# A two-layer streaming encoder step: both halves of the normalised tokens kept in DRAM, gate blocks tied to the state steps, and the last third of the modulation product moved into the state stage

## The chip, the cores and the metric

The kernel runs on one core of one Trainium2 chip. The metric is the device time of one launch in microseconds, as the median of several runs. A profiled execution shows in addition what each engine did: PE is TensorE (matmul), PEld its weight load, DVE is VectorE, ACT is ScalarE, POOL is GpSimd, and SP is SyncE, which here only issues transfers. A transfer can also be issued from ACT's or POOL's own instruction stream.

## The reference: what is computed

2176 tokens (a prompt of 2048, and 8 samples of 16) of width 1024 go through two layers in float32. Each layer computes

```
mod = silu(c) @ w_ada[i] + b_ada[i]        # shift, scale, gate of 1024 each; 9 rows of c
h   = rms_norm(x, norm_g[i]) * (1 + scale) + shift
x   = x + gate * branch_i(h)
```

Layer 0 is a diagonal complex state-space branch (S5): `u, z = split(h @ w_in)`; u goes through a complex recurrence (64 groups of 16 channels, 64 states each), then a GELU, a gated product `y * sigmoid(y @ w_glu + b)`, a multiplication by `silu(z)`, and `@ w_out`. Layer 1 is a gated delta rule on chunks of tokens, with a short convolution ahead of it and a gated output product behind it. A last RMSNorm ends the step. z is called the gate half here: its columns of `w_in` are the second 1024.

## The kernel before

**Split products.** A float32 matrix product is made of three matmuls at the faster float32r rate: every operand is split into a high part (a rounding copy, by ACT) and a low part (the difference, by DVE), and `mm3` (L145 to L152) issues high times high, high times low, low times high (lines L149, L150, L151). Some small products stay in plain float32: the modulation product `ada`, and in the state stage the transposes `abT`, the kernels `pk`, the inputs `pb` and the Toeplitz part of `py`.

**Tiling.** Tokens are cut into 8 blocks of 272 columns (`NCH`). Weights are cut into 8 output blocks of 128 columns, each holding 8 tiles of 128x128. One output block of one token block is 8 x 3 = 24 matmuls of 128x128 by 128x272.

**Stages**, in time order. In stage A, for each token block j, the tokens are loaded, normalised, modulated and split into the tiles `hh` and `hl`; 8 output blocks of u (`pd`) are computed and stored to `u_d`. The normalised and modulated tokens `xt` themselves are stored to `h0_d` in one transfer. Stage A also computes the modulation product: the 6144 columns are done in three groups of 2048 (`ada0`, `ada1`, `ada2`), each in 8 steps over the 1024 rows of `w_ada` (`ada_steps`, L172). A step has four matmuls of 128x32 by 128x512, one for each quarter of the group's columns, and each writes another 32 rows of one PSUM tile, through another quarter of the PE array (`tile_position=(0, 32 * j)`).

In stage B, the S5 recurrence runs in 16 state steps b (four channel groups each: `s5_setup`, `s5_load`, `s5_main`): PE makes `abT`, `pk`, `pb` and `py`, and a long chain of DVE instructions between `pb` and `py` does the rotations and scans. The 64 gate blocks (8 token blocks times 8 output blocks; `z_block`, `pdz`) are written behind the state steps in the program. Their tokens come back from `h0_d` by `load_h0`: a transfer into the staging tile `hz` (one buffer), an ACT copy and a DVE subtraction into `hhz` and `hlz` (L230, three buffers each; one token block uses two of each).

Stage C does the gated product (`pg`), the product with `w_out` (`po`) and the second normalisation; then come the convolution and input products of layer 1 (`pc`, with blockwise solves that use `pdg`), its gate products (`pz`), and the chunked delta rule.

**What sets the order.** Except where a block of code is marked as ordered, a scheduler decides at build time in which order the instructions stand on each engine: it plays the program against its own estimate of durations, takes what is ready, and prefers what the program wrote first. The order is then fixed: each engine works through its list, and waits at an instruction whose inputs are not there. `later([i])` and `issue_after(i)` forbid an instruction to stand ahead of instruction i. Gate blocks 58 to 63 are held back in this way until the last state step's `py`; blocks 0 to 57 are free.

Of the kernel before, what the change touches and what calls it, by code (L numbers as in the profile page):

```python
# [18 lines left out]
P = 128  # L19
# [34 lines left out]
def kernel(ctx: ExitStack, tc: tile.TileContext, I, O, upto="Z"):  # L54
# [30 lines left out]
    h0_d = [dr.tile([D, NCH], F32, name=f"h0_d{i}") for i in range(8)]  # L85
# [86 lines left out]
    def ada_steps(gi, pool, pps, mpool, mtag):  # L172
        c0, acc = gi * 2048, []

        def step(k):
            wt = []
            for i in range(2):
                t = pool.tile([P, D], F32, tag="r", name=f"wa{gi}_{k}_{i}")
                l, col = divmod(c0 + i * D, 3072)
                nc.sync.dma_start(t, I["w_ada"][l, k * P:(k + 1) * P, col:col + D])  # L180
                wt += [t[:, 0:512], t[:, 512:1024]]
# [39 lines left out]
    xz = pab.enter_context(tc.tile_pool(reuse_waits="tile", name="xz", bufs=1))  # L221
    psd = pab.enter_context(tc.tile_pool(reuse_waits="tile", name="psd", bufs=2, space=PSUM))
    psa = pab.enter_context(tc.tile_pool(reuse_waits="tile", name="psa", bufs=1, space=PSUM))

    spl = {}

    def split_x(nm, xt, hf):
        a = hp.tile([P, 4, NCH], F32R, tag="hh", name=f"hh{nm}_{hf}")
        b = hp.tile([P, 4, NCH], F32R, tag="hl", name=f"hl{nm}_{hf}")
        spl["i"] = [S.copy(a, xt).ins, V.tensor_sub(b, xt, a.bitcast(F32)).ins]  # L230
        return ks(a, 4), ks(b, 4)

    with ExitStack() as pa:
# [47 lines left out]
        def apply_mod(j, xt, first=False):  # L281
# [4 lines left out]
            for hf in range(2):  # L286
                k4 = range(4 * hf, 4 * hf + 4)
                if not first:
# [3 lines left out]
                    hl.append(split_x(j, xt[:, 4 * hf:4 * hf + 4], hf))  # L292
                    continue
# [7 lines left out]
                hl.append((ks(a, 4), ks(b, 4)))  # L301
            (h0, l0), (h1, l1) = hl
            nc.scalar.dma_start(h0_d[j].rearrange("(k p) n -> p k n", p=P), xt)
            return h0 + h1, l0 + l1
# [50 lines left out]
        def first_scale(k, mA):  # L355
# [8 lines left out]
            i_ = S.activation(hk[:, 0:NPC], xk, AF.Identity, scale=gs0[:, k, 0:1], bias=modT[:, k, 0:1])  # L364
# [4 lines left out]
            spl["i"] = [V.tensor_sub(lk, xcur[:, k], hk.bitcast(F32)).ins, i_.ins]  # L369
# [60 lines left out]
        nc.scalar.dma_start(h0_d[0].rearrange("(k p) n -> p k n", p=P), xcur)  # L430
# [139 lines left out]
        ada = ada_steps(1, wr, psa, sp1, "sq") + ada_steps(2, wr, psa, sp1, "sq")  # L570
        for j in range(8):
            hh, hl = hcur
            T.ordered = j == 1
            for cb in range(8):
# [20 lines left out]
                if j > 1 and cb % 3 == 1:  # L595
# [14 lines left out]
    def load_h0(j):  # L610
        hh, hl = [], []
        for hf in range(2):
            xt = xz.tile([P, 4, NCH], F32, tag="x", name=f"hz{j}_{hf}")
            nc.sync.dma_start(xt, h0_d[j][512 * hf:512 * hf + 512].rearrange("(k p) n -> p k n", p=P))
            a, b = split_x(f"z{j}", xt, hf)
            hh, hl = hh + a, hl + b
# [18 lines left out]
    with ExitStack() as pb:  # L635
# [7 lines left out]

        stN = b1.tile([P, 32, 2, 8], F32, name="stN")
# [1439 lines left out]
```

## Time and profile before

| | |
|---|---|
| median of 3 runs | 2159.88 us (2156.17 to 2161.8) |
| profiled execution, own time | 2161.6 us |
| its span | 2159.9 us |
| PE busy | 2087.7 us, 97% of the span |
| DVE busy | 1565.3 us, 72% |
| ACT, POOL busy | 973.2 us (45%), 474.5 us (22%) |
| moved by DMA | 332.40 MB, mean 154 GB/s |
| last `pd` of stage A, first `pdz` | 271.7 us, 272.2 us |
| last `py` of the state steps | 601.3 us |
| first `pg` of stage C | 621.8 us |

A matmul's end is modelled, so that neighbouring matmuls overlap in the records: what a matmul costs PE in a dense stretch is read from start to start. A plain float32 matmul shows up as two records, and as one row of the program's order.

### The profile page before, as it was taken

The numbers are of one execution on the slowest core, as the hardware profiler recorded it, in microseconds if no ns is written. First come the engines' busy times: TensorE is split into PE (matmuls) and PEld (weight loads), VectorE is DVE, ScalarE is ACT, GpSimd is POOL, SyncE is SP. The second block draws the span as 40 slices with busy tenths as digits, with TensorE's granted clock in tenths as the row PEclk, the third lists the DMA queues.
The fourth block names the chain that finished last, engine by engine and source line by source line (L and its number), as shares of the span: only waits on it lengthen the run. The fifth ranks groups of instructions, "written<-read, shape, count | busy, mean of one in ns | idle before, by whom it ended". The sixth has DMA issues, their size and how long they took to land. (4 is left out here: it accounts for less than half of the span.)

```text
span 2159.9 us, 42182 instructions
## 1 busy us (share of the span) xinstructions
PE 2087.7 (97%) x15729; PEld 1854.0 (86%) x15729; DVE 1565.3 (72%) x4013; ACT 973.2 (45%) x2289; POOL 474.5 (22%) x725
## 2 busy tenths in 40 slices
PE   6999999999799999999999999999999899999998
PEld 4889888888589999999888879889887688888887
DVE  6999598999856544446665669687546888888875
ACT  3543433333255444446665422341224566666663
POOL 1157510000112222221100010100011234444430
PEclk7999999999799999999999999999999899999999
DMA  9797854454284333336565212573456644444432
GB/s 277 237 303 245 249 150 141 142 162 148 95 243 149 107 112 107 110 99 227 145 203 169 80 53 70 142 177 92 137 165 215 190 134 132 133 144 146 146 112 69
DMA packets 395209, 332.40 MB, mean 154 GB/s; under 512 B 88026, under 2 KB 358890, under 8 KB 395004
## 3 DMA queue, kind: packets, MB, share of 16 engines
q1 hardware_dynamic: 259084, 226.56, 35.7%
q10 hardware_dynamic: 133104, 95.49, 13.8%
q0 software_dynamic: 2816, 7.65, 1.0%
q8 instruction: 124, 2.03, 0.4%
q14 instruction: 81, 0.66, 0.1%
HBM read 213.01 MB, written 116.61 MB: 153 GB/s over the span
## 5 line engine op out<-in xcount | busy, mean ns | idle before, releaser
L149 PE MATMUL pc<-h1h,wdh 128*128 128x512 f32 (+1 forms) x600 | 216.2, 361 | 0.0
L151 PE MATMUL pc<-h1h,wdl 128*128 128x384 f32 (+1 forms) x600 | 216.2, 360 | 0.0
L150 PE MATMUL pc<-h1l,wdh 128*128 128x384 f32 (+1 forms) x600 | 215.2, 359 | 0.5 <-POOL h1l L1344 0.5
L1404 DVE SCALAR_TENSOR_TENSOR ac<-pb,convw,ac 128x384 f32<-128x384 f32 (+3 forms) x288 | 164.1, 594 | 3.4
L150 PE MATMUL pdz<-hlz,wzh 128*128 128x272 f32 x512 | 152.3, 298 | 0.0
L149 PE MATMUL pdz<-hhz,wzh 128*128 128x272 f32 x512 | 151.6, 297 | 0.7 <-ACT evz L630 0.7
L149 PE MATMUL pg<-yh,wgh 128*128 128x272 f32 x512 | 148.2, 290 | 3.5 <-ACT evz L630 3.5
L151 PE MATMUL pdz<-hhz,wzl 128*128 128x272 f32 x512 | 150.9, 295 | 0.0
L149 PE MATMUL po<-gh,woh 128*128 128x272 f32 x512 | 148.2, 290 | 1.1 <-ACT gh L937 1.1
L150 PE MATMUL pg<-yl,wgh 128*128 128x272 f32 x512 | 149.1, 291 | 0.0
L151 PE MATMUL pg<-yh,wgl 128*128 128x272 f32 x512 | 148.3, 290 | 0.0
L151 PE MATMUL po<-gh,wol 128*128 128x272 f32 x512 | 147.9, 290 | 0.0
L150 PE MATMUL po<-gl,woh 128*128 128x272 f32 x512 | 147.1, 288 | 0.0
L149 PEld LDWEIGHTS pc<-h1h,wdh 128*128 128x128 f32 x600 | 113.1, 188 | 12.0 <-issue 1.7
L150 PEld LDWEIGHTS pc<-h1l,wdh 128*128 128x128 f32 x600 | 113.0, 188 | 10.9 <-POOL h1l L1344 0.8
L151 PEld LDWEIGHTS pc<-h1h,wdl 128*128 128x128 f32 x600 | 113.0, 188 | 10.4 <-issue 0.8
L149 PE MATMUL pd<-hh,wuh 128*128 128x272 f32 x384 | 112.7, 294 | 0.1
L69 PE MATMUL epo<-w2h,ohi 128*128 128x512 f32 x272 | 111.5, 410 | 0.0
L150 PE MATMUL pd<-hl,wuh 128*128 128x272 f32 x384 | 110.8, 289 | 0.3 <-DVE hl L230 0.3
L151 PE MATMUL pd<-hh,wul 128*128 128x272 f32 x384 | 110.9, 289 | 0.0
L69 PE MATMUL epo<-w2h,olo 128*128 128x512 f32 x272 | 106.9, 393 | 0.0
L69 PE MATMUL epo<-w2l,ohi 128*128 128x512 f32 x272 | 106.9, 393 | 0.0
(617 smaller groups left out, 6334.3 us busy)
## 6 DMA issues: line engine op xcount, KB each, us to landing
wa<-in_w_ada SPq DMA_DIRECT2D x32, 512.0 KB
wdr<-in_w_in SPq DMA_DIRECT2D x24, 512.0 KB
h_d<-x ACTq DMA_DIRECT2D x8, 1088.0 KB
u_d<-ev ACTq DMA_DIRECT2D x64, 136.0 KB
hz<-h_d SPq DMA_DIRECT2D x16, 544.0 KB
u<-u_d SPq DMA_DIRECT2D x16, 544.0 KB
z_d<-evz ACTq DMA_DIRECT2D x64, 136.0 KB
y_d<-y ACTq DMA_DIRECT2D x32, 272.0 KB
```

What stands on the lines that cost most here:

```text
L69: i_ = f(*a, **kw)
L149: T.matmul(ps, lhsT=w_hi[k], rhs=x_hi[k], start=(k == 0), stop=False)
L150: T.matmul(ps, lhsT=w_hi[k], rhs=x_lo[k], start=False, stop=False)
L151: i_ = T.matmul(ps, lhsT=w_lo[k], rhs=x_hi[k], start=False, stop=(k == n - 1))
L1404: V.scalar_tensor_tensor(o, src(j), convw[:, b, j:j + 1], o, op0=ALU.mult, op1=ALU.add)
```

## The change

1. **Both parts are kept.** `h0_d` becomes two DRAM tensors for each token block. Stage A stores the tiles `hh` and `hl` (four transfers of 544 KB for each token block, from ACT's stream) in place of `xt` (one of 1088 KB). `load_h0` loads both parts straight into `hhz` and `hlz`: four transfers in place of two, and no copy and no subtraction. The staging pool `xz` is gone.
2. **The last modulation group** (`ada2`) moves from stage A into stage B, with weight tiles of 512 columns in a pool of two buffers: each of its 8 steps has four loads of 256 KB in place of two of 512 KB. In stage A the first two output blocks of every three that carried a step still do (two steps for each token block, not three).
3. **Gate blocks are tied to the state steps.** Gate block n, from 8 on, may not stand ahead of the first `pb` group of state step `n * 16 // 58 - 1`.
4. **Later stages.** The four `kt` tiles of a blockwise solve are loaded at its start, ahead of the `ra` rows, into four buffers in place of two. Two transposed rows of the modulation (`pg9`) get a PSUM buffer of another pool (`psh` in place of `pso`).

```diff
     def ada_steps(gi, pool, pps, mpool, mtag, n=D):
...
-            for i in range(2):
-                t = pool.tile([P, D], F32, tag="r", name=f"wa{gi}_{k}_{i}")
...
+            for i in range(2 * D // n):
+                t = pool.tile([P, n], F32, tag="r", name=f"wa{gi}_{k}_{i}")
...
+    def keep_h0(j, hf, ab):
+
+        for w in range(2):
+            nc.scalar.dma_start(h0_rows(j, w, hf), ab[w].bitcast(F32))
...
-            nc.scalar.dma_start(h0_d[j].rearrange("(k p) n -> p k n", p=P), xt)
...
-        ada = ada_steps(1, wr, psa, sp1, "sq") + ada_steps(2, wr, psa, sp1, "sq")
+        ada = ada_steps(1, wr, psa, sp1, "sq")
...
-                if j > 1 and cb % 3 == 1:
+                if j > 1 and cb in (1, 4) and ada:
...
     def load_h0(j):
         hh, hl = [], []
         for hf in range(2):
-            xt = xz.tile([P, 4, NCH], F32, tag="x", name=f"hz{j}_{hf}")
-            nc.sync.dma_start(xt, h0_d[j][512 * hf:512 * hf + 512].rearrange("(k p) n -> p k n", p=P))
-            a, b = split_x(f"z{j}", xt, hf)
-            hh, hl = hh + a, hl + b
+            ab = [hp.tile([P, 4, NCH], F32R, tag="h" + i, name=f"h{i}z{j}_{hf}") for i in "hl"]
+            for w in range(2):
+                nc.sync.dma_start(ab[w].bitcast(F32), h0_rows(j, w, hf))
+            hh, hl = hh + ks(ab[0], 4), hl + ks(ab[1], 4)
...
+        ada = ada_steps(2, ps5.enter_context(tc.tile_pool(reuse_waits="tile", name="adp", bufs=2)), psa, b1, "abt", 512)
...
+                steps.append(i_.ins)
...
+            if b > 2 and ada:
+                ada.pop(0)()
...
-            with later([ends[zst["n"] > 58]] if zst["n"] > 57 else []):
+            n = zst["n"]
+            with later([ends[n > 58]] if n > 57 else [steps[2 * (n * 16 // 58 - 1)]] if n > 7 else []):
                 z_block()
...
-        l2 = pl_.enter_context(tc.tile_pool(reuse_waits="tile", name="l2", bufs=2, side="right"))
+        l2 = pl_.enter_context(tc.tile_pool(reuse_waits="tile", name="l2", bufs=4, side="right"))
...
+            kts = [load_k(t) for t in ts]
...
-            pt = pso.tile([P, 512], F32, tag="o", name=f"pg9{hf}")
+            pt = psh.tile([P, 512], F32, tag="h", name=f"pg9{hf}")
```

The program's order shows what became of it. First the modulation product on PE. Before, each of its 8 steps of group 2 stands in stage A as two rows of two matmuls, so four neighbours on the four quarters of the array (`ada2_3100`, between the u blocks `pd7_1` and `pd7_2`):

```order
L151 MATMUL pd7_1_3756<-hh7_1_3551,wul1_202 128x272
L186 MATMUL ada2_3100<-wa2_6_0_3784,cs_176 32x512 x2
L186 MATMUL ada2_3100<-wa2_6_1_3786,cs_176 32x512 x2
L149 MATMUL pd7_2_3792<-hh7_0_3543,wuh2_199 128x272
L150 MATMUL pd7_2_3792<-hl7_0_3544,wuh2_199 128x272
```

In the change, at the start of stage B, the third and the fourth matmul of step 0 (`wa2_0_2`, `wa2_0_3`) stand among the matmuls of gate block 1 of token block 0 (`pdz0_1`):

```order
L151 MATMUL pdz0_1_6372<-hhz0_0_6336,wzl1_3989 128x272
L149 MATMUL pdz0_1_6372<-hhz0_0_6336,wzh1_3988 128x272
L150 MATMUL pdz0_1_6372<-hlz0_0_6337,wzh1_3988 128x272
L186 MATMUL ada2_4660<-wa2_0_2_4656,cs_184 32x512
L151 MATMUL pdz0_1_6372<-hhz0_0_6336,wzl1_3989 128x272
L149 MATMUL pdz0_1_6372<-hhz0_1_6340,wzh1_3988 128x272
L150 MATMUL pdz0_1_6372<-hlz0_1_6341,wzh1_3988 128x272
L690 MATMUL abT0_4080<-ident_168,abt0_4072 128x128 x4
L151 MATMUL pdz0_1_6372<-hhz0_1_6340,wzl1_3989 128x272
L149 MATMUL pdz0_1_6372<-hhz0_1_6340,wzh1_3988 128x272
L186 MATMUL ada2_4660<-wa2_0_3_4658,cs_184 32x512
L150 MATMUL pdz0_1_6372<-hlz0_1_6341,wzh1_3988 128x272
```

What was a pack of four now stands one by one: the 32 matmuls of the group form 29 separate places, 3 of them with two, and 22 of the 29 have float32r matmuls on both sides. All stand ahead of the `py` of state step 5. Over the whole of stage B, PE's row of instructions changes from float32r to plain float32 and back at 87 places before, and at 127 with the change; one of these is the transpose of the finished group and 22 are lone `ada2` places, so that 17 more come from the state steps' own pieces.

Second, PE near the end of the state steps, around the last `pb` (step 15, in two groups `pb15_0` and `pb15_1`). Before:

```order
L151 MATMUL pdz7_1_7963<-hhz7_1_7763,wzl1_4033 128x272
L775 MATMUL py14_0_6128<-u14_5899,toe14_5940 128x272
L775 MATMUL py14_1_6129<-u14_5899,toe14_5940 128x272
L735 MATMUL pb15_0_6172<-u15_6033,ab15_6046 64x272 x4
L735 MATMUL pb15_1_6181<-u15_6033,ab15_6046 64x272 x4
L780 MATMUL py14_0_6128<-xsh14_6123,cah14_5926 128x272
L780 MATMUL py14_1_6129<-xsh14_6123,cah14_5926 128x272
```

With the change:

```order
L151 MATMUL pdz6_7_7940<-hhz6_1_7564,wzl7_3976 128x272
L784 MATMUL py14_0_6192<-u14_5963,toe14_6004 128x272
L784 MATMUL py14_1_6193<-u14_5963,toe14_6004 128x272
L743 MATMUL pb15_0_6236<-u15_6097,ab15_6110 64x272 x4
L149 MATMUL pdz7_0_7968<-hhz7_0_7792,wzh0_3990 128x272
L150 MATMUL pdz7_0_7968<-hlz7_0_7793,wzh0_3990 128x272
L151 MATMUL pdz7_0_7968<-hhz7_0_7792,wzl0_3991 128x272
```

Gate blocks 56 and 57 (`pdz7_0`, `pdz7_1`) stood ahead of `pb15_0`, and now stand behind it. Counted in gate blocks that stand ahead of the first `pb` of a step, it was 14.6 at step 3, 34.2 at step 8, 51.8 at step 13 and 58.0 at step 15; now it is 12.8, 33.0, 49.7 and 56.0.

Third, SP's list at the blockwise solves 1 and 2 of the convolution stage. Before, `kt9` to `kt11` stand behind the 16 loads of `ra1`:

```order
L1643 DMA ra1_16393<-row_d_159 32x8x32 x16
L1653 DMA kt9_17057<-kq_d_124 128x512
L1653 DMA kt10_17108<-kq_d_124 128x512
L133 DMA wdr2048_17451<-in_w_in1 128x8x128
L1653 DMA kt11_17159<-kq_d_124 128x512
```

With the change they stand directly behind `kt8`:

```order
L1656 DMA kt8_16956<-kq_d_132 128x512
L1656 DMA kt9_16958<-kq_d_132 128x512
L1656 DMA kt10_16960<-kq_d_132 128x512
L1656 DMA kt11_16962<-kq_d_132 128x512
```

The 16 loads of `ra1` (the rows of solve 1) now come five rows behind `kt11`; `kt8` to `kt11` are the tiles of solve 2.

45 lines of the change are left out of this document (26 added, 19 removed).

## The prediction

> **What bounds the kernel now.** The page first: PE is busy for almost the whole span.
>
> ```profile
> span 2159.9 us, 42182 instructions
> PE 2087.7 (97%) x15729; PEld 1854.0 (86%) x15729; DVE 1565.3 (72%) x4013; ACT 973.2 (45%) x2289; POOL 474.5 (22%) x725
> ```
>
> A change that moves work is therefore worth what it does to PE's own time, unless it fills one of PE's few holes. The busy time of each engine by stretch shows where those are (stretch, its length, PE, PEld, DVE, ACT and POOL busy, then PE's granted clock, DMA share and GB/s).
>
> ```profile
> 102.00:272.00 170.00, 169.55 (x1304) 151.81 (x1304) 136.12 (x651) 68.11 (x122) 100.85 (x276) 1.00 0.80 261
> 272.00:340.00 68.00, 67.55 (x532) 58.61 (x530) 62.91 (x138) 23.11 (x55) 5.95 (x15) 1.00 0.48 145
> 340.00:534.00 194.00, 194.00 (x1493) 161.17 (x1492) 180.02 (x380) 67.77 (x167) 2.98 (x20) 1.00 0.49 152
> 555.00:602.00 47.00, 35.75 (x201) 26.30 (x200) 33.98 (x57) 11.42 (x28) 7.53 (x9) 0.71 0.34 109
> 602.00:622.00 20.00, 15.79 (x122) 15.14 (x121) 7.97 (x7) 9.46 (x15) 0.00 (x0) 1.00 0.83 244
> 622.00:627.00 5.00, 5.00 (x29) 5.00 (x30) 2.11 (x3) 3.31 (x5) 0.47 (x1) 0.66 1.02 313
> ```
>
> Stage A (to 272) and the state stage up to 534 have no hole: PE lacks 0.45 us in 170, 0.45 in 68 and nothing in 194. VectorE is close behind it in the state stage (180 of 194), but not first. The holes are in 555 to 602, the last two state steps, where PE is idle for 11.3 us and runs at a mean clock of 0.71, and at the passage to stage C. PE's waits from 555 to 622 name them:
>
> ```profile
> PE py L780 <- ACT xsh L129: 5.9, 2, 5.6
> PE pg L149 <- ACT evz L630: 3.5, 1, 3.5
> PE pb L735 <- DVE f L740: 2.5, 1, 2.5
> ```
>
> The gate blocks are PE's filler. Their evictions (first row) and the `pb` records (16 for each state step, second row), counted between 340 and 534, and the evictions after 555 (third), show how they are spread today:
>
> ```profile
> 340.00:534.00 194.00, 14.30 (x37) 1.00 0.49 152
> 340.00:534.00 194.00, 24.75 (x160) 10.24 (x160) 25.79 (x40) 3.70 (x20) 0.00 (x0) 1.00 0.49 152
> 555.00:602.00 47.00, 1.16 (x3) 0.71 0.34 109
> ```
>
> That is 37 gate blocks for 10 state steps, 3.7 for each, where an even spread over 16 gives 58/16 = 3.6. The spread is even already, but for the end: 3 blocks in the last 47 us. So tying blocks to steps has little to even out.
>
> **Stage A: eight packs leave.** One pack of four `ada` matmuls and its neighbours:
>
> ```profile
> 111.78 0.29 PE L150 MATMUL pd<-hl,wuh 128*128 128x272 f32 x1
> 111.91 0.29 PE L151 MATMUL pd<-hh,wul 128*128 128x272 f32 x1
> 112.12 1.07 PE L186 MATMUL ada<-wa,cs 128*32 128x512 f32 x8
> 113.12 0.40 PE L150 MATMUL pd<-hl,wuh 128*128 128x272 f32 x1
> 113.35 0.29 PE L151 MATMUL pd<-hh,wul 128*128 128x272 f32 x1
> ```
>
> From 111.91 to 113.35 are 1.44 us, in which two ordinary steps of 0.13 would stand, so the pack costs 1.19: 1.00 for its eight records and 0.19 for going to plain float32 and back. PE has no hole there, so 8 x 1.19 = **-9.5 us**.
>
> **Stage B: the same product one by one.** The trace has no lone 128x32 matmul of 512 columns. The nearest row is the full-width one (two of them as four records, and the next instruction):
>
> ```profile
> 1658.59 1.88 PE L1251 MATMUL sp<-vm,kup 128*128 128x512 f32 x4
> 1660.40 0.21 PE L1145 MATMUL epx<-xf,qt 32*32 32x32 f32 x1
> ```
>
> Two take 1.81, one 0.91. The pack's four took 1.00 together, so its members run side by side and the columns that stream through set the time; alone, each should pay that time for itself. The order has 29 places: 29 x 0.91 = 26.4, and 22 of them change the mode on both sides: 22 x 0.19 = 4.2. The 17 further changes of mode among the state steps' pieces add 17 x 0.19 = 3.2. **+33.8 us**, in a stretch (272 to about 400) without a hole. Bounds: if a lone quarter-width matmul costs a quarter of the pack, 0.25, it is 29 x 0.25 + 7.4 = 14.7; if the three pairs don't run side by side either, 36.5. I take 33.8, since the rows price columns streamed, not array filled. The Trainium skill speaks against the scattering too: by "TensorEngine Tiling (Array Packing)", Key Properties, a change of tiling mode drains TensorE, and only different tiles run in parallel; the 0.19 around the pack agrees with such a drain.
>
> **The spread: two blocks.** Ahead of the last step's `pb` stand 56 gate blocks, not 58. A block is 24 matmuls at 0.126 (from 617.40 to 618.03 below are five steps), 3.0 us; PE comes to that point 2 x 3.0 earlier and does them in the hole behind: **-6.1 us**.
>
> ```profile
> 617.40 0.29 PE L149 MATMUL pdz<-hhz,wzh 128*128 128x272 f32 x1
> 618.03 0.29 PE L151 MATMUL pdz<-hhz,wzl 128*128 128x272 f32 x1
> 621.83 0.40 PE L149 MATMUL pg<-yh,wgh 128*128 128x272 f32 x1 [3.51 <-ACT evz L630]
> ```
>
> The rest of the hole is the last step's chain on VectorE. No filler shortens it: ahead of the `py` that starts at 592.23, VectorE's scans and rotations fill the time (PE and DVE rows of the timeline, joined in order of time).
>
> ```profile
> 583.65 0.42 PE L780 MATMUL py<-xsh,cah 64*128 64x272 f32 x1
> 583.88 0.42 PE L780 MATMUL py<-xsl,cah 64*128 64x272 f32 x1
> 584.56 2.71 DVE L749 TENSOR_TENSOR_SCAN z<-rN,cy,z 128x128 f32<-128x128 f32 x4
> 587.31 2.36 DVE L763 TENSOR_TENSOR t<-z,tw 128x1024 f32<-128x1024 f32 x2
> 592.23 0.59 PE L780 MATMUL py<-xsh,cah 64*128 64x272 f32 x2 [5.59 <-ACT xsh L129]
> 595.61 0.43 PE L151 MATMUL pdz<-hhz,wzl 128*128 128x272 f32 x1
> 595.84 0.43 PE L149 MATMUL pdz<-hhz,wzh 128*128 128x272 f32 x1
> ```
>
> What filler can save is the half clock: behind the chain, `pdz` stepped at 0.23, not 0.126, and `py` likewise, so that some 29 matmuls took 0.10 too long each. With more filler I count that as won: **-3.0 us** (bounds 0, and -8.2 with the other 5.2 of the 11.3 idle gone too). By the Trainium skill, "TensorE: Matmul & The Clock Gate", HAM oscillation, gaps of more than about 3.4 us are what brings the half clock; here `py` stepped at 0.23 at 583.65 already, ahead of the 5.59 gap and behind gaps of 2.5 at most, so the trace doesn't hold to that limit.
>
> **Copy and subtraction gone.** 16 subtractions and as many ACT copies leave the state stage:
>
> ```profile
> L230 DVE TENSOR_TENSOR hlz<-hz,hhz x16: 1270/1288/1350, 234.1 to 554.4; 128x1088 fp32r<-128x1088 f32 x16
> ```
>
> 16 x 1.29 = 20.6 us of VectorE. PE has no wait there that this could end, so I count nothing; it is cover in case VectorE becomes the bound. The stores double by 8.9 MB in stage A, where 8.4 MB of weights leave at a DMA share of 0.80; stage B gets 17.3 MB in 350 us, 50 GB/s on 150 at a share of 0.49. Nothing while this stays cover. ACT issues 24 more stores, in a stage where it is busy for 68 of 170 us.
>
> **The two late places.**
>
> ```profile
> 1402.98 0.34 PE L150 MATMUL pc<-h1l,wdh 128*128 128x384 f32 x1
> 1407.54 0.49 PE L1657 MATMUL pdg<-kt 128*32 128x32 f32 x32 [4.23 <-DMA kt<-kq_d]
> 1407.00:1412.00 5.00, 4.33 (x76) 4.13 (x77) 5.00 (x9) 1.54 (x2) 0.00 (x0) 0.66 0.88 278
> 1564.98 0.50 PE L149 MATMUL pz<-h1h,wdh 128*128 128x512 f32 x1 [1.54 <-ACT g L1717]
> ```
>
> This `kt` is late because it stands behind the 16 `ra` rows in SP's list. It now stands ahead of them: the 4.2 us go, and with them the half clock behind (5 us at 0.66, 5 x 0.34 = 1.7). **-5.9 us**; nothing, if SP meets another late transfer. The wait for `g` ends with its PSUM buffer: **-1.5 us** (or 0).
>
> **Sum.** -9.5 + 33.8 - 6.1 - 3.0 - 5.9 - 1.5 = +7.8. The passage to stage C (3.51 us, and 5 us at 0.66) hangs on ACT's order behind a weight transfer, as before: 0, between -5.2 and +3. The profiled execution took 2161.6 us, 1.7 above the median of 2159.9; 2161.6 + 7.8 = 2169.4, and beside the median 2167.7, so **2168 us**, with a range of its own of 2162 to 2175.
>
> **Rival 1, faster: lone quarter-width matmuls are cheap.** If PE lets a float32r matmul begin in the other quarters, or a record of 32 columns streams faster, the 33.8 becomes 14.7 and the sum -11.3: 2149. The sum falls below -6.5 once a place costs under about 0.42. Against it: 1.00 for the pack is not less than the full-width 0.91. For it: no row shows one alone.
>
> **Rival 2, no change: the stage packs without a hole.** The VectorE time set free lets the last steps keep up, the remaining 5.2 us of idle vanish, and the passage to stage C loses its 3.5 and 1.7: 7.8 - 10.4 = -2.6, 2157. Against it: the chain above is VectorE's, without a subtraction in it.
>
> **Rival 3, slower: SP's list.** Doubled token loads and 32 weight loads share SP's one list with what the steps need. A token block's second half can only be loaded when its buffer is free, near the end of the block before.
>
> ```profile
> 387.55 0.37 SPq L614 DMA_DIRECT2D hz<-h_d  x1
> 391.64 1.10 ACT L230 CAST hhz<-hz 128x1088 fp32r<-128x1088 f32 x1 [1.93 <-DMA hz<-h_d]
> ```
>
> 4.1 us from issue to use for one part; with the second behind it about 6. In between PE has the block's first 12 matmuls (1.5 us) and some state work. At 3 us for each of 7 passages: +21 more, 2189. It decides once the wait is longer than the state work that stands there.
>
> **How the numbers follow.** A measurement of this kernel tells 0.3%, 6.5 us, from no change: 2153.4 to 2166.4 is the same. Forecast 0.45 (a third of it below 2166.4), rival 1 0.17, rival 2 0.20 (a tenth of it faster), rival 3 0.18. Slower: 0.30 + 0.18, and 0.02 for waits in other stages: 0.50; same: 0.15 + 0.18 - 0.02 = 0.31; faster: 0.17 + 0.02 = 0.19. The range takes in rival 1's price and most of the way to rival 3's: 2148 to 2185.
>
> **What would show it.** In the changed profile: `ada` at L186 as pairs of records with about 0.9 us from its first record to the next matmul (0.25 for rival 1); `pd` to `pdz` some 9.5 us earlier; the last `py` of the state steps some 15 us later than 601.3; a mean clock near 1 in the last 47 us of the steps; PE waits on `hhz` or `hlz` for rival 3; no wait on `kt` and `g`. The forecast is wrong if the time from the first `pdz` to the first `pg` grows by less than 15 us or by more than 35.

## The result, and the profile after

| | before | changed |
|---|---|---|
| median | 2159.77 us (2156.17 to 2161.8) | 2197.84 us (2194.74 to 2200.62) |
| ratio to before, 95% interval | | 1.0166, [1.0145, 1.0187] |
| profiled execution, span | 2159.9 us | 2193.9 us |

The change makes the kernel 38 us slower. The direction was forecast, the size was not: 2168 us was predicted, with a range up to 2185. The first lines of the page of the changed kernel:

```profile
span 2193.9 us, 42213 instructions
PE 2118.8 (97%) x15729; PEld 1863.3 (85%) x15729; DVE 1547.7 (71%) x3997; ACT 954.8 (44%) x2273; POOL 477.5 (22%) x725
```

PE issues as many matmuls as before (15729), but is busy for 31.1 us longer; VectorE and ScalarE have less to do. So most of the loss is not waiting: the same matmuls cost PE more. Where that happens is seen when both traces are cut at the same events. "Opening" is everything up to the first `pd` at L149, the first matmul of token block 2 (the ordered code before it shows up as L69). Stage A goes from there to the first `pdz`, stage B to the first `pg`, stage C to the last `po`, the convolution to the last `pc` at L149. All kernels of this study stand in the table, each from its one profiled execution; the experiments below refer to it.

| kernel | opening | A | B | C | conv. | rest | ratio to before |
|---|---|---|---|---|---|---|---|
| before | 102.1 | 170.1 | 349.6 | 392.6 | 429.9 | 715.6 | |
| changed | 112.0 | 163.2 | 383.1 | 394.8 | 425.2 | 715.7 | 1.0166 [1.0145, 1.0187] |
| 1 modulation back in stage A | 113.7 | 171.8 | 347.8 | 393.7 | 426.1 | 715.0 | 1.0028 [1.0011, 1.0044] |
| 2 modulation in packs | 113.2 | 167.1 | 348.5 | 392.4 | 424.5 | 716.4 | 0.9989 [0.9978, 1.0] |
| 3 block 0's stores held | 118.0 | 164.8 | 389.0 | 393.0 | 424.8 | 714.7 | 1.0193 [1.0175, 1.0211] |
| 4 the same, early loads held | 117.3 | 165.9 | 383.4 | 393.8 | 425.5 | 717.5 | 1.0182 [1.0153, 1.0211] |
| 5 stores on GpSimd | 108.4 | 160.8 | 385.7 | 394.3 | 425.7 | 714.4 | 1.0124 [1.0099, 1.015] |
| 6 the same, half the bytes | 104.3 | 160.7 | 380.5 | 393.6 | 426.0 | 715.5 | 1.0079 [1.0063, 1.0094] |
| 7 packs, GpSimd, loads held | 107.2 | 166.1 | 348.9 | 393.1 | 424.9 | 721.3 | 0.9975 [0.9961, 0.9988] |
| 8 kept parts alone | 113.9 | 171.8 | 356.5 | 392.3 | 431.9 | 713.7 | 1.0089 [1.0075, 1.0103] |
| 9 binding alone | 102.5 | 170.1 | 351.4 | 392.3 | 432.5 | 717.0 | 1.0025 [1.0015, 1.0036] |
| 10 changed, not bound | 112.0 | 164.6 | 390.2 | 394.0 | 426.8 | 715.0 | 1.0177 [1.0163, 1.0191] |
| 11 packs, not bound (one program with 2) | 111.4 | 162.2 | 354.3 | 392.7 | 424.9 | 716.7 | 0.9987 [0.9978, 0.9996] |
| 12 late places alone | 101.9 | 170.1 | 349.7 | 392.8 | 426.9 | 717.0 | 0.9978 [0.9967, 0.9989] |
| 13 packs, blocks 0 and 1 as before | 101.6 | 161.0 | 341.7 | 394.9 | 425.2 | 713.8 | 0.9908 [0.9893, 0.9924] |
| 14 the same, not bound (one program with 13) | 102.0 | 161.0 | 342.6 | 393.7 | 425.2 | 714.1 | 0.9897 [0.9878, 0.9915] |

The 34.0 us of the two spans are +9.9 in the opening, -6.9 in stage A, +33.5 in stage B, +2.2 in stage C, -4.7 in the convolution and nothing behind it.

The stretches of one execution have a spread of their own. The kernels of rows 2 and 11 build to one and the same program, and so do those of 13 and 14. Yet between rows 2 and 11 the opening differs by 1.8, stage A by 4.9 and stage B by 5.8 us, while the sum of the three differs by 0.9. A difference of that size between two rows shows nothing by itself.

**Stage B.** The busy time by stretch at its start, at its end and at the passage to stage C (columns as in the prediction):

```profile
275.00:380.00 105.00, 103.91 (x651) 70.12 (x650) 74.73 (x166) 23.98 (x64) 9.13 (x23) 1.00 0.59 187
592.00:640.00 48.00, 39.20 (x247) 30.83 (x244) 31.81 (x55) 11.46 (x28) 9.12 (x8) 0.79 0.49 150
639.00:659.00 20.00, 17.24 (x137) 16.66 (x134) 8.41 (x7) 10.49 (x16) 0.00 (x0) 0.97 0.73 214
```

In the first row PE is full, but with 651 matmuls in 105 us, 6.2 for each us; in the prediction's row for the start of this stage (272 to 340) there were 532 in 68, 7.8 for each. PE is busy with something that takes longer. One of the lone `ada2` places, from the timeline of PE:

```profile
282.17 0.29 PE L149 MATMUL pdz<-hhz,wzh 128*128 128x272 f32 x1
282.38 1.04 PE L186 MATMUL ada<-wa,cs 128*32 128x512 f32 x2
283.36 0.39 PE L150 MATMUL pdz<-hlz,wzh 128*128 128x272 f32 x1
283.59 0.29 PE L151 MATMUL pdz<-hhz,wzl 128*128 128x272 f32 x1
```

From 282.17 to 283.59 are 1.42 us. Two ordinary steps would take 0.25, so the place costs 1.17: 0.98 for one matmul that fills a quarter of the array's columns, and 0.19 for the change to another piece of the array and back. The waits of PE in stage B:

```profile
PE py L789 <- ACT xsh L129: 7.0, 1, 7.0
PE pg L149 <- ACT evz L637: 2.5, 1, 2.5
PE pdz L149 <- DMA hhz<-h0h_d: 2.2, 1, 2.2
PE pb L743 <- DMA u<-u_d: 1.5, 1, 1.5
```

The wait for `xsh` in the last state step is still there. The wait for `hhz` is new, and the one for `u` was 0.4 before.

**The opening.** Two of ScalarE's waits up to 120 us stand out. The kernel before has the first at 3.8 us, and not the second:

```profile
ACT ev L69 <- DMA u_d<-ev: 7.5, 1, 7.5
ACT L459 <- DMA wa<-in_w_ada: 6.1, 1, 6.1
```

The timeline of ScalarE shows what stands at the first (ACTq rows are transfers that ScalarE issues, from the start of the row to the issue):

```profile
79.57 0.37 ACTq L237 DMA_DIRECT2D h0h_d<-hh  x1
79.64 0.39 ACT L69 COPY ev<-pd 128x272 f32<-128x272 f32 x1
80.03 1.01 ACTq L237 DMA_DIRECT2D h0l_d<-hl  x1
81.14 0.70 ACTq L237 DMA_DIRECT2D h0h_d<-hh  x1
81.93 4.38 ACTq L320 DMA_DIRECT2D u_d<-ev  x5
87.14 0.38 ACTq L237 DMA_DIRECT2D h0l_d<-hl  x1
87.56 0.39 ACT L69 COPY ev<-pd 128x272 f32<-128x272 f32 x1 [7.53 <-DMA u_d<-ev]
87.84 1.12 ACT L69 ACTIVATE sq<-x 128x1088 f32<-128x1088 f32 x1
```

Nine stores stand in a row, four of them of the kept parts, and ScalarE computes nothing for 7.5 us; the `sq` of a later token block starts at 87.84 in place of 79.35. Before, six stores stand there. The order of the program shows why a store can hold its engine: besides its data it waits for one of a few numbered transfer semaphores, so for an older transfer that used the same one.

```
L237 DMA h0h_d_81<-hh_0_712 128x4x272 [waits DMAHW3_49,Activation_49]
L237 DMA h0l_d_82<-hl_0_713 128x4x272 [waits DMAHW4_49,DVE_49]
L237 DMA h0h_d_81<-hh_1_726 128x4x272 [waits DMAHW5_49,Activation_49]
L320 DMA u_d_65<-ev_2_740 128x272 [waits DMAHW6_49,Activation_49]
```

### The profile page after: what moved, and what is told of

Its sections match the earlier page's. It is cut to its first block, busy times and chain, and to the rows that moved or that the text cites. A ratio compares the mean times of both kernels' runs of the same rounds, so it can differ in the third digit from the quotient of the medians.

```text
span 2193.9 us, 42213 instructions
## 1 busy us (share of the span) xinstructions
PE 2118.8 (97%) x15729; PEld 1863.3 (85%) x15729; DVE 1547.7 (71%) x3997; ACT 954.8 (44%) x2273; POOL 477.5 (22%) x725
## 5 line engine op out<-in xcount | busy, mean ns | idle before, releaser
L149 PE MATMUL pc<-h1h,wdh 128*128 128x512 f32 (+1 forms) x600 | 216.5, 361 | 0.6 <-ACT pb L1406 0.6
L149 PE MATMUL pdz<-hhz,wzh 128*128 128x272 f32 x512 | 154.0, 301 | 2.5 <-DMA hhz<-h0h_d 2.2
L149 PE MATMUL pg<-yh,wgh 128*128 128x272 f32 x512 | 148.1, 289 | 2.5 <-ACT evz L637 2.5
L149 PE MATMUL po<-gh,woh 128*128 128x272 f32 x512 | 148.7, 291 | 0.4 <-ACT gh L950 0.3
L149 PEld LDWEIGHTS pc<-h1h,wdh 128*128 128x128 f32 x600 | 112.6, 188 | 12.8 <-issue 1.7
L151 PEld LDWEIGHTS pc<-h1h,wdl 128*128 128x128 f32 x600 | 112.6, 188 | 10.2 <-issue 0.8
L149 PE MATMUL pd<-hh,wuh 128*128 128x272 f32 x384 | 113.7, 298 | 3.5 <-ACT hh L227 3.5
L149 PEld LDWEIGHTS pdz<-hhz,wzh 128*128 128x128 f32 x512 | 97.0, 190 | 22.1 <-issue 15.6
L69 PE MATMUL epo<-w2h,ohi 128*128 128x512 f32 x272 | 111.6, 410 | 0.0
L69 PE MATMUL epo<-w2h,olo 128*128 128x512 f32 x272 | 106.9, 393 | 0.0
```

Source lines behind the costliest of these rows:

```text
L69: i_ = f(*a, **kw)
L149: T.matmul(ps, lhsT=w_hi[k], rhs=x_hi[k], start=(k == 0), stop=False)
L151: i_ = T.matmul(ps, lhsT=w_lo[k], rhs=x_hi[k], start=False, stop=(k == n - 1))
```

## The experiments

Ratios and stretches stand in the table above; each ratio is against runs of the kernel before that were made beside it. That kernel's median was 2159.8 us beside the changed kernel, and 2164 to 2165 us beside the experiments, and most expected totals were worked out from the first figure. So across the two, ratios are to be compared, not medians.

### Is it the lone matmuls? (1 and 2)

Experiment 1 puts the last modulation group back:

```diff
-        ada = ada_steps(1, wr, psa, sp1, "sq")
+        ada = ada_steps(1, wr, psa, sp1, "sq") + ada_steps(2, wr, psa, sp1, "sq")
...
-                if j > 1 and cb in (1, 4) and ada:
+                if j > 1 and cb % 3 == 1:
...
-            if b > 2 and ada:
-                ada.pop(0)()
```

> The changed kernel with the last third of the modulation weights put back into stage A (packs of four full-width matmuls there, 1024-column loads); the kept parts, the tying of the gate blocks, the early `kt` loads and `pg9` stay. Theory 'scatter' (the 32 lone `ada` matmuls and the changes of tiling they force are what made stage B 33.5 us longer): the stretch from the first `pdz` to the first `pg` falls from 383.1 to 350-356 us, the stretch from the first `pd` of stage A to the first `pdz` grows from 163.2 to 170-173 us, and the opening loses the 1.4 us that it waits for delayed loads of `wa`; total 21 to 27 us under the changed kernel, 2171-2177 us. Rival 'tie' (binding the gate blocks to the state steps, with their doubled loads, made stage B longer): the stretch from `pdz` to `pg` stays at 375 us or more and the total stays at 2190 us or more.

Stage B fell by 35.3 us to 347.8, a little more than expected, and stage A grew by 8.6 to 171.8; the median was 2170.5. The opening did not shorten (113.7), so the early `ada2` loads were not what made it long. PE's time from start to start in stage B, without its idle time, fell from 365.9 to 331.2 us, by 34.7. Up to the last state step's first `pb`, where the clock is full in both, it fell by 31 us for the same number of gate blocks. So the scattered group costs 31 to 35 us there, as theory 'scatter' said. With the binding and the doubled loads, which stayed, stage B is no longer than before (349.6).

Experiment 2 leaves the group in stage B, in the same 4 KB of buffer, but as packs:

```diff
...
+        def half(k, h):
+            t = adp.tile([P, 4, 256], F32, tag="r", name=f"wa2_{k}_{h}")
+            nc.sync.dma_start(t, I["w_ada"][1, k * P:(k + 1) * P, 1024:3072]
+                              .rearrange("p (j h n) -> p j h n", j=4, h=2)[:, :, h])
+            for j in range(4):
+                T.matmul(adt[32 * j:32 * j + 32, 256 * h:256 * h + 256], lhsT=cs[:, k, :], rhs=t[:, j],
+                         start=(k == 0), stop=(k == KC - 1), tile_position=(0, 32 * j))
...
```

> The changed kernel with the last third of the modulation weights still in stage B, but in packs: one load brings four column groups of 256 columns (the same 4 KB per partition), and its four matmuls stand next to each other in four column groups, so 16 packs of half width in place of 32 lone matmuls of full width. Nothing is left out. Theory 'scatter': a pack of half width costs about 0.5 us and a change of tiling of 0.19 us, with as much again for some of the pieces that it pushes away, 16 x 0.7 to 0.9 = 11 to 14 us in place of 32; the stretch from the first `pdz` to the first `pg` falls from 383.1 to 361-366 us, total 2176-2182 us. Rival 'tie': that stretch stays at 375 us or more.

Stage B took 348.5 us, 34.6 under the changed kernel and 13 to 17 us under what was expected. One pack in the timeline:

```profile
302.71 0.64 PE L660 MATMUL ada<-wa,cs 128*32 128x256 f32 x8
303.28 0.39 PE L149 MATMUL pdz<-hhz,wzh 128*128 128x272 f32 x1
```

These are four matmuls in 0.57 us. One of the 16 packs was still torn in two, so that the group stands in 17 places, which took 9.7 us together. The sum of columns and products is that of the 32 lone matmuls. Some 13 us of the gain are in the last state steps: behind the last step's first `pb`, PE had 3.8 gate blocks (11.5 us) more to do than in the changed kernel and took 1.4 us less. The clock now stays full there (third number from the end of the row):

```profile
560.00:605.00 45.00, 42.92 (x323) 36.34 (x322) 32.19 (x55) 12.78 (x31) 7.61 (x9) 1.00 0.53 166
```

### What makes the opening longer? (3 to 7)

The first theory was the place of block 0's stores: two of them stand in the middle of the opening on ScalarE's list, ahead of `un` (the second of the two waits above).

```diff
-        for hf in range(2):
-            keep_h0(0, hf, [t[hf] for t in h0])
+        with later([S.last, V.last]):
+            for hf in range(2):
+                keep_h0(0, hf, [t[hf] for t in h0])
```

> The changed kernel with the four stores of token block 0's parts bound behind the last ScalarE and VectorE instruction of the opening; nothing else. Theory 'list' (the two stores of the first half that stand in the middle of the opening on ScalarE's list made it wait 6.1 us, and the half clock followed): the first `pd` of stage A starts at 103-106 us in place of 112.0, the 6.1 us wait on ScalarE ahead of `un` and the 4.9 us wait on VectorE behind it are gone, total 6 to 9 us under the changed kernel, 2189-2192 us. Rival 'loads' (the two early `ada2` loads on SP's list are the cause): the first `pd` stays at 110 us or later and the total stays within 2 us of the changed kernel.

The theory fell: the wait ahead of `un` is gone, and yet the opening took 118.0 us, 6.0 more than in the changed kernel. The timeline of ScalarE:

```profile
77.42 4.22 ACTq L320 DMA_DIRECT2D u_d<-ev  x5
81.73 0.60 ACTq L237 DMA_DIRECT2D h0l_d<-hl  x1
82.37 0.39 ACT L69 COPY ev<-pd 128x272 f32<-128x272 f32 x1 [6.87 <-DVE sm L479]
82.40 0.78 ACTq L237 DMA_DIRECT2D h0h_d<-hh  x1
89.00 0.37 ACTq L237 DMA_DIRECT2D h0l_d<-hl  x1
91.85 0.37 ACTq L237 DMA_DIRECT2D h0h_d<-hh  x1
93.00 1.11 ACT L69 ACTIVATE sq<-x 128x1088 f32<-128x1088 f32 x1 [10.24 <-issue]
```

The stores only moved to where others already stood, and `sq` came at 93.0 in place of 87.8. Holding the early `ada2` loads back as well changed little:

```diff
             if b > 2 and ada:
-                ada.pop(0)()
+                with later([xl]):
+                    ada.pop(0)()
```

> The changed kernel with the stores of block 0 held as in the kernel with held stores, and the `ada2` steps bound behind the load of the last token block, so that their first two loads leave the opening's part of SP's list. Theory 'list': the first `pd` of stage A starts at 102-103.5 us (before: 102.1), 1 to 2 us earlier than with the stores held alone; total 8 to 10 us under the changed kernel, 2188-2190 us; stage B as in the changed kernel, 380-385 us. Rival 'loads': most of the 10 us come only here and not with the stores held alone.

117.3 us: 0.7 us for the loads, and neither theory right. So the next try took the eight stores of blocks 0 and 1 off ScalarE's list altogether:

```diff
-            nc.scalar.dma_start(h0_rows(j, w, hf), ab[w].bitcast(F32))
+            (nc.gpsimd if j < 2 else nc.scalar).dma_start(h0_rows(j, w, hf), ab[w].bitcast(F32))
```

> The changed kernel with the stores of both parts of token blocks 0 and 1 issued by GpSimd in place of ScalarE, so that none of the eight stands on ScalarE's list; the other blocks' stores stay on ScalarE. Holding block 0's stores back did not shorten the opening but made it 6 us longer (first `pd` of stage A at 118.0 us), and there ScalarE stood from the last copy of `ev` at 75.5 to the first `sq` at 93.0 us in stores. Theory 'stores on ScalarE' (wherever they stand on its list, each of the eight stores holds ScalarE for its issue and for an older transfer whose semaphore it takes, where before there were two): the first `pd` of stage A falls from 112.0 to 102-105 us, total 6 to 10 us under the changed kernel. Rival 'traffic' (the opening is longer because of the doubled bytes or the early loads, whoever issues them): the first `pd` stays at 109 us or later. Stage B is not touched by either: 380-390 us from the first `pdz` to the first `pg`.

The total fell by 0.42% (9 us) as expected, but the opening only to 108.4: 3.6 of the 9.9 come back there, less than the theory asked for, and 2.4 in stage A, which is less than the 4.9 by which stage A differs between rows 2 and 11. What is left shows in the DMA share (next to last column) of the stretch from 74 to 92 us. Before, changed, and with the stores on GpSimd:

```profile
74.00:92.00 18.00, 18.00 (x142) 17.84 (x141) 16.46 (x120) 7.61 (x15) 0.00 (x0) 1.00 1.00 342
```

```profile
74.00:92.00 18.00, 18.00 (x131) 17.92 (x131) 13.38 (x95) 8.56 (x20) 0.00 (x0) 0.90 1.07 364
```

```profile
74.00:92.00 18.00, 14.75 (x115) 14.42 (x113) 10.67 (x76) 6.14 (x14) 2.43 (x3) 1.00 1.04 400
```

The DMA engines are full in this stretch even before the change. In the changed kernel the four stores of block 1 are issued in it, where before there was one of half their bytes, so that something must be pushed back. Experiment 6 keeps the GpSimd stores and leaves out the low parts of blocks 0 and 1:

```diff
-        for w in range(2):
+        for w in range(1 if j < 2 else 2):
...
```

> The kernel with the stores of blocks 0 and 1 on GpSimd, and of these two blocks only the high parts are stored: as many bytes in the opening as the kernel before stores (2.18 MB), in place of 4.35. Left out: the low parts of the gate half of blocks 0 and 1, which are read from block 2's store instead (the output of those tokens is then not the reference's; loads and matmuls of stage B are as many as before). There the opening took 108.4 us to the first `pd` of stage A, with the DMA engines busy throughout 74 to 92 us in this kernel and in the one before. Theory 'bytes' (what is left of the longer opening is the 2.18 MB more in that stretch, at 0.34 to 0.4 MB per us 5.4 to 6.4 us): the first `pd` falls to 102-104 us, total 4 to 6 us under the kernel with the GpSimd stores (2189.5), 2183-2186 us. Rival 'order' (what is left comes from the early `ada2` loads and the order of the lists): the first `pd` stays at 107 us or later, total within 2 us of it.

104.3 us: another 4.1, just above what 'bytes' had worked out (102 to 104). GpSimd also has four stores fewer to issue, and that was not told apart from their bytes. The total fell by 8.7 us between the two medians. In the profiles 5.2 of it stand in stage B, which neither theory had spoken of, and which differs by as much between rows 2 and 11. Experiment 7 joins the packs, the GpSimd stores and the held loads:

> The changed kernel with both cures: the last third of the modulation weights in packs of four column groups of 256 columns (2162.3 us alone), the stores of blocks 0 and 1 issued by GpSimd, and the first loads of that third bound behind the load of the last token block. Theory 'stores on ScalarE': the 10 us of the opening come off, 2151-2155 us, 0.4 to 0.65% under the kernel before. Rival 'traffic': 2159-2163 us.

The median was 2158.1 us, between the two expectations, with 107.2 for the opening. The profiled execution spent 5 us more than the others behind the convolution (721.3), so that its span (2161.5) is no better than that of the packs alone; the medians differ by 4.2 us.

### The parts alone (8, 9 and 12)

Experiment 8 makes edit 1 of the change alone, both parts kept for all eight blocks:

> The kernel before with both parts kept for all eight blocks alone (no binding, modulation weights all in stage A, late loads as before). Theory 'the kept parts cost the opening and nothing else': the first `pd` of stage A at 110-114 us, stage A 170 to 172 us, stage B from the first `pdz` to the first `pg` 347-351 us, total 2168-2174 us. The prediction had put this edit at zero: 2157-2163 us. A rival by which the doubled loads of the gate half cost stage B: 354 us or more there, total 2175 us or more.

The opening (113.9) and stage A (171.8) are as the first theory had them; stage B is 6.9 us above before, which it had not. Stage B and the median, 2182.3 us (18 us above before), are in the range of the rival, but its mechanism is the smaller part: PE's waits on `hhz` and `hlz` are 1.9 us together. The large waits in stage B, and the busy time of the last state steps:

```profile
PE pb L742 <- DVE f L748: 8.5, 1, 8.5
PE py L788 <- ACT xsh L129: 6.5, 2, 5.2
```

```profile
583.00:625.00 42.00, 24.38 (x111) 16.57 (x108) 30.19 (x52) 8.28 (x20) 8.34 (x8) 0.59 0.38 117
```

PE is idle for 17.6 us of these 42, at a clock of 0.59, where the kernel before lost 11.3 in 47. All 58 free gate blocks are done when the last state step begins, and 57.3 already at the one before (55.8 before the change). So with the kept parts the gate blocks run ahead, and the hole that they should fill grows: from the last step's first `pb` to the first `pg` it is 56.4 us, and 52.4 before. (This stretch repeats well: in rows 2 and 11 it is 52.0 in both, and it lies between 52.4 and 53.5 in the changed kernel and experiments 3 to 6, which have the same gate blocks ahead of each step.) That it was the copy and the subtraction that had held the blocks back is likely, but was not shown apart.

Experiment 9 binds the gate blocks and does nothing else:

> The kernel before with the binding of the gate blocks to the state steps alone. Theory of the prediction (two blocks moved into the hole of the tail take 6.1 us out of it and the half clock behind it 3.0): 2151-2155 us. Rival 'binding alone moves nothing' (with no scattered loads and the modulation weights in stage A the binding gave 347.8 us of stage B against 349.6): within 3 us of the kernel before, and the wait of PE on `xsh` in the tail still 5 us or more.

It is 0.25% slower (4.2 us between the medians), not faster. The rival is right, but for its 3 us, and PE's wait on `xsh` is 11.5 us in one piece in place of 5.6 and some smaller ones.

Experiment 12 makes only edit 4:

> The kernel before with the early loads of `kt` (four buffers) and `pg9` in its other pool alone. The prediction's two terms: -5.9 us in the convolution (first to last: 430 to 424 us between the last `po` and the last `pc`) and -1.5 us behind it, 2151-2155 us. Rival 'only the loads' (the convolution took 425-426 us with it in every kernel so far and the rest 714-717 us as before): 2154-2157 us, the rest unchanged.

The median is 4.4 us lower (0.9978); the convolution gave 3.0 in the profile (426.9), and the rest none (717.0), as the rival had it.

### Does the binding do anything? (10 and 11)

With the kept parts in the kernel the binding has something to hold. Experiment 10 takes it from the changed kernel, 11 from the packed one:

```diff
-            with later([ends[n > 58]] if n > 57 else [steps[2 * (n * 16 // 58 - 1)]] if n > 7 else []):
+            with later([ends[n > 58]] if n > 57 else []):
```

> The changed kernel without the binding of the gate blocks to the state steps (only the last two blocks held back, as in the kernel before); the lone matmuls of the last third stay in stage B. In the profiles so far the hole of the tail went with the number of gate blocks that are done when the last state step begins: 58.0 (before; 57.8 with the binding alone), 58.0 (kept parts alone), 56.0 (changed kernel), 55.7 (modulation back in stage A), 52.2 and 53.0 (packs, bound or not). Theory 'binding' (the kept parts let the gate blocks run ahead, and only the binding holds them): 57.5 or more blocks done, the waits and the half clock of the tail as with the kept parts alone, stage B 390-394 us, total 2204-2210 us. Rival 'loads in the stage' (modulation matmuls between the state steps hold the gate blocks back by themselves, bound or not): 56.5 blocks or fewer, stage B within 4 us of 383.1, total 2194-2201 us.

> The changed kernel with the packs, and without the binding of the gate blocks to the state steps (only the last two blocks are held back, as in the kernel before). Theory 'binding fills the tail' (the end of stage B at clock 1.00, with 9.2 us of idle PE in place of 15.9, is the binding's work): without it the blocks are used up before the last state steps, the half clock of the tail returns, the stretch from the first `pdz` to the first `pg` grows from 348.5 to 354-360 us, total 6 to 12 us above the packed kernel, 2168-2174 us. Rival 'packs fill the tail' (it is the order in which the packs push the gate blocks back that does it): within 3 us of the packed kernel, 2159-2165 us.

Unbound, the changed kernel's stage B grew by 7.1 us to 390.2, with 58.0 gate blocks done when the last step begins and this wait, the one of the kept parts alone:

```profile
PE pb L743 <- DVE f L749: 9.9, 1, 9.9
```

From the last step's first `pb` to the first `pg` it takes 57.4 us in place of 53.4, although PE has two gate blocks less to do there. The two totals are not clearly apart (1.0177 against 1.0166, with intervals that overlap).

Experiment 11 settles its question for the rival more firmly than a time could: with the packs, the bound and the unbound kernel are one program, since the order keeps to the binding without being told to. So 0.9987 against 0.9989, the 5.8 us that stage B is longer, and the 6.7 us that opening and stage A are shorter, are what two executions of one program differ by. Both have 52.2 gate blocks done when the last step begins, and no hole. So with lone matmuls the binding is worth some 4 us at the end of stage B, and with packs it does nothing at all. Why packs in the list hold the gate blocks back and lone matmuls do not was not settled: it is the build's order that decides it.

### The best version (13 and 14)

Experiment 13 has the packs and the held loads, and keeps blocks 0 and 1 as the kernel before does, so that the opening has its old stores and bytes. In stage B they are split in place:

```diff
...
+            if j < 2:
+                nc.sync.dma_start(ab[1].bitcast(F32), h0_rows(j, 0, hf))
+                S.copy(ab[0], ab[1].bitcast(F32))
+                V.tensor_sub(ab[1], ab[1].bitcast(F32), ab[0].bitcast(F32))
-            for w in range(2):
+            for w in range(2 if j > 1 else 0):
...
```

> The kernel with the packs and the held loads, in which blocks 0 and 1 are kept as the kernel before keeps them (one store each of the unsplit block, split again in stage B, in place); both parts are kept from block 2 on. Theory 'stores and bytes of the opening': ScalarE's list, stores and bytes of the opening are the old ones, so the first `pd` of stage A starts at 102-104 us, and with stage B at 349-351 us and the convolution at 424-426 us the total is 2150-2155 us, 0.45 to 0.7% under the kernel before. Rival 'order': the opening stays at 107 us or more, total 2157-2162 us.

The opening is back (101.6), and with stage A it ends 9.7 us earlier than before, about what the prediction's first term had for stage A. The median is 2144.4 us, 20 us or 0.92% under before, where 0.45 to 0.7% was expected: stage B took 341.7 (and 342.6 in experiment 14), not 349 to 351. Why it is shorter than with the packs alone was not shown. The end of the state steps and PE's waits there:

```profile
545.00:585.00 40.00, 38.63 (x291) 32.60 (x290) 30.68 (x52) 11.07 (x28) 7.51 (x8) 1.00 0.55 171
```

```profile
PE pg L149 <- ACT evz L641: 4.2, 1, 4.2
PE py L803 <- ACT y L812: 1.4, 1, 1.4
```

PE is idle for 1.4 us of these 40, and the wait on `xsh` is gone. Experiment 14 is the same without the binding:

> The best version so far (packs, blocks 0 and 1 kept as before, held loads; ratio 0.9908) without the binding of the gate blocks. Theory 'binding': some 5 us of stage B come back, ratio 0.9925-0.994. Rival 'loads in the stage': the same within 0.15%, 0.989-0.9925, with 52 to 54 gate blocks done when the last state step begins.

The ratio is 0.9897 against 0.9908, and 53.0 gate blocks are done in both when the last step begins. As with 2 and 11 this is one program, run twice. Both runs are faster than the kernel before and the changed one, and the binding is not what they owe it to.

## Why the prediction was right in direction and wrong in size

It had +7.8 us for the span, and the profile shows +34.0. Its own steps, one by one (predicted, then measured):

- **Stage A, -9.5: -6.9.** Taking the packs out gave 8.6 (171.8 to 163.2, experiment 1 against changed). The kept parts seem to cost 1.7 there (experiment 8 against before), which "Nothing while this stays cover" had put at 0. That is less than stage A differs by between rows 2 and 11.
- **Scattered `ada2`, +33.8: right in sum, and partly by luck.** Up to the last step's first `pb`, PE's time from start to start grew by 28.2 us with two gate blocks (6.0) fewer in it: 34.2. Experiment 1 gives 31 for the group alone up to there. Two errors in the term partly cancel. A place costs 0.98, not 0.91: the 28 places in stage B took 27.4. And the 0.19 belongs to a change to another piece of the array and back, not to one of number format (shown at the end): up to that `pb` there are 50 more changes of piece, so 25 there and back, 4.8 us, where 39 changes of format were priced at 7.4. "Columns streamed, not array filled" was the right reading of the full-width row, and rival 1 is out: 0.98 for a lone matmul, not 0.25.
- **The spread and the half clock, -6.1 and -3.0: about half came.** The 56 blocks ahead of the last step are there, as read from the order. From that `pb` to the first `pg` PE had 6.0 us more to do and took 1.0 us longer, so some 5 of 9.1 were gained. The half clock stayed: 0.79 over the last 48 us of the steps, where "With more filler I count that as won" had 3.0. Two blocks did not close the hole; the 11 to 12 that were left in experiments 2 and 13 did. Rival 2, by which the hole would close, is out too: PE was idle for 8.8 of these 48 us.
- **"Copy and subtraction gone ... I count nothing": this step failed, in two places.** The first is the opening, which the prediction did not look at: it grew by 9.9 us, and by 11.8 with the kept parts alone. The working compared the stores' bytes with a DMA share averaged over stage A (102 to 272 us), and ACT's 24 more stores with ACT's busy time there. But the eight stores of the first two blocks are issued ahead of that stretch, four of them in 74 to 92 us, where the DMA engines were already full, and on a list where a store holds ScalarE until an older transfer lands. Taking the stores off ScalarE's list gave back 3.6 us, and halving their bytes 4.1. Holding the early loads gave 0.7 and 1.2, and about 1 is left over; both are within the 1.8 by which the openings of rows 2 and 11 differ. With the old stores and bytes, and the loads held, the opening is back at 101.6 (experiment 13). The second place is stage B, where the kept parts let the gate blocks run ahead, so that the hole grows (experiment 8: +4.0 behind the last step's first `pb`, and +6.9 for the whole stage). It may be that the removed work had been of use where it stood; that was not shown apart. The binding won those 4 us back (experiment 10), so that against the kernel before it gained little.
- **Rival 3, SP's list: its mechanism is there, at a fifth of its price.** Ahead of the last step PE's idle time grew from 1.4 to 5.7 us, with the 2.2 us wait on `hhz` and the 1.5 on `u`; it had put 21 on this. The forecast's own sum had 0.
- **`kt`, -5.9: -4.7.** The wait fell from 4.2 to 0.8:

```profile
PE pdg L1677 <- DMA kt<-kq_d: 0.8, 1, 0.8
```

- **`g`, -1.5: 0.** The wait is gone, and the stretch behind the convolution is as long as before (715.7); PE's waits on `qt` in the delta rule went from 1.4 to 3.1 us. A wait of one engine removed was not time won.
- **Passage to stage C, 0:** the wait fell by 1.0 (3.5 to 2.5), and stage C took 2.2 us more, with a half clock from 688 to 692 us that was not there before. Why, stays open.

So 9.9 of the 26.2 us that were missed are the opening, 8.8 stage B (4.1 in the two terms of the hole, 4.3 in new waits), 2.6 stage A, and 4.9 small differences elsewhere. The bound that the prediction gave itself for failure, more than 35 us from the first `pdz` to the first `pg`, was not reached (33.5): stage B was judged nearly right, and the cost outside it was not searched for.

By the Trainium skill, "TensorEngine Tiling (Array Packing)", Key Properties, a change of tiling mode drains TensorE and different tiles can run in parallel. The 0.19 around a lone matmul, and 0.98 us for one lone matmul against 0.57 for four of half its columns, agree with it.

## What to carry to other kernels

Here a lone matmul that fills a quarter of the array's columns cost PE 0.98 us, and a full one 0.91, so work moved in between other work should move as whole packs. Loading all that a pack needs in one transfer, half as wide since the buffer is small, kept 15 of 16 packs whole in experiment 2 and 13 of 16 in the best version. Before extra transfers are booked as free, look at the stretch in which they are issued, not at an average over the stage behind it: its DMA share, and the list of the engine that issues them. Work removed from a second engine isn't always free to remove: with the kept parts, the filler that the end of the stage needed was used up earlier. And before a line is credited with a gain, see whether it changes the program at all: with the packs the binding did not, and two executions of one program differed by 5.8 us in one stage.

## What the runs showed of the hardware

- In the changed kernel a step to a matmul on another piece of the array (128*128, 64*128 or 128*32 in the rows, which print f32 for both formats) cost more time, and a change of number format alone did not. Between 280 and 560 us the median step from a `pdz` matmul (float32r, full array) to the next `pdz` is 0.125 us. To `py` from `toe` (plain float32, full array) it is 0.125 too. To `py` from `xsh` (float32r, 64 rows) and to a lone `ada` (plain float32, 32 columns) it is 0.216. From the end of the steps:

```profile
603.80 0.29 PE L151 MATMUL pdz<-hhz,wzl 128*128 128x272 f32 x1
603.93 1.08 PE L784 MATMUL py<-u,toe 128*128 128x272 f32 x4
613.14 0.28 PE L150 MATMUL pdz<-hlz,wzh 128*128 128x272 f32 x1
613.35 0.40 PE L789 MATMUL py<-xsh,cah 64*128 64x272 f32 x2
```

- Stores on a compute engine's list can hold that engine for long: 7.5 us without an instruction of ScalarE's own for nine stores (changed kernel), 10.2 us at one place with block 0's stores held back.
- The half clock can come after a short gap. In the changed kernel it is there from some 616 us on, as PE's timeline and the busy time of 616 to 622 us show:

```profile
615.98 0.72 PE L784 MATMUL py<-u,toe 128*128 128x272 f32 x2 [1.08 <-ACT y L793]
616.94 0.42 PE L789 MATMUL py<-xsl,cah 64*128 64x272 f32 x1
617.17 0.42 PE L789 MATMUL py<-xsh,cal 64*128 64x272 f32 x1
```

```profile
616.00:622.00 6.00, 6.00 (x18) 4.32 (x19) 5.98 (x7) 1.01 (x3) 5.76 (x7) 0.56 0.77 235
```

  The steps take 0.23 us, and the clock is 0.56. It was 1.00 from 608 to 616, and the gap of 1.08 us is PE's longest listed wait from 590 to 622, so the clock fell before the 7.0 us wait at 623. The Trainium skill, "TensorE: Matmul & The Clock Gate", HAM oscillation, ties the half clock to gaps of more than about 3.4 us; this trace does not bear out such a limit.
